# Spilled tiles fetched by ScalarE into eight buffers of their own, gate products held two tiles back, early row gathers dropped

## The chip, the core and the metric

The kernel runs on one core of a Trainium2 chip. The metric is device time in microseconds (us) of one execution. The profile of an execution gives a span (first to last instruction) and, for each engine, what it did and what it waited for. Engines are named as the profile names them: PE (TensorE), ACT (ScalarE), DVE (VectorE), POOL (GpSimd) and SP (SyncE, which only issues transfers here).

## What is computed

Two transformer layers on 256 tokens of width 1024, in float32. Each layer has a mixing part (convolution, windowed attention, grouped attention; not touched here) and a feed-forward part that looks up experts:

```python
def peer_ffn(h, w_q, sub_keys, u, v):
    ...
        idx = jnp.take_along_axis(cand_i.reshape(PEER_CHUNK, PEER_HEADS, n_cand), best_pos, axis=-1)
        g = jax.nn.softmax(best_s, axis=-1).astype(xc.dtype)
        act = jax.nn.gelu(jnp.einsum('cd,chkd->chk', xc, jnp.take(u, idx, axis=0)))
        return jnp.einsum('chk,chkd->cd', g * act, jnp.take(v, idx, axis=0))
```

Each token uses 8 x 16 = 128 of 16384 experts; `u` and `v` are 16384 x 1024. Layer 0 has 512 tokens in this part (256 of x and 256 of the context), layer 1 has 256.

## The kernel before

**Dense and gathered tokens.** Tokens are handled in tiles of 128. In layer 0 three of the four token tiles are dense: for them all 16384 experts are computed, with a gate that is zero for an expert that was not chosen. The fourth tile gathers its experts' rows instead. In layer 1 both tiles are dense and nothing is gathered.

**Expert tiles.** The 16384 experts are 128 expert tiles, numbered e. For each there is an up gemm (`act`: a 128x1024 piece `u` times the tokens, 24 matmuls into a PSUM bank `psu`, then gelu on ACT into a tile `gact`) and a down gemm (`sweep`: activation times gate, then times a piece `v`, into PSUM banks `acc` that stay open over all 128 tiles; 18 matmuls of 512 columns in layer 0, 12 in layer 1). Every operand is split in a high and a low part to keep float32 accuracy: ACT copies the high part (`hi_u`, `hi_v`, `whi`), DVE or POOL subtracts to get the low part (`lo_u`, `lo_v`, `wlo`), and three matmuls replace one.

**Spilling.** While DVE still works out the routing and the gates, PE runs the up gemms of the first tiles. The first 4 (layer 0) or 8 (layer 1) stay in SBUF. The next 42 or 32 are written to DRAM (`spilled`), and the sweep reads them back as `gback`. So in layer 0 tiles 4 to 45, and in layer 1 tiles 8 to 39, come back in the sweep and need no up gemm there; from tile 46 (40) on, up and down gemms alternate.

**The gates.** `gd` in DRAM holds the gates; a block `gr` with the gates of 8 tiles is fetched by ACT's queue, two buffers. `gr0_40` is the block for tiles 40 to 47 of layer 0. In layer 0 a block is 1536 KB in pieces of 512 bytes. The product of activation and gate is the DVE operation on line 793 (`wi` in the code).

**The gathered tile.** `gather_steps` makes a list of 259 steps: 128 gathers of rows of `u` by POOL's queue (`gru`) with a dot product each on DVE, then 128 gathers of rows of `v` (`grv`), each of 512 KB. Each gather is held until a given instruction has run.

**Order.** A scheduler orders the instructions of each engine from the program and its own estimates; each engine then runs its list strictly in order. A DMA is issued by the engine whose list it stands in, and that engine waits there until the DMA's buffer is free.

Of the kernel before, what the change touches and what calls it, by code (L numbers as in the profile page):

```python
# [11 lines left out]
F32 = mybir.dt.float32  # L12
# [5 lines left out]
AF = mybir.ActivationFunctionType  # L18
ALU = mybir.AluOpType
AX = mybir.AxisListType  # L20

P = 128
# [20 lines left out]
EG = 8  # L43
GA = {0: 4, 1: 8}
SPILL = {0: 42, 1: 32}
GEARLY = 8
GLAG = 3
WOV = {0: (0, 1), 1: (1, 1)}
ZAT = (0, 2, 4, 6, 7, 9)
GE0 = 20  # L50


@with_exitstack
def hymba_kernel(ctx: ExitStack, tc: tile.TileContext, a, out):
    nc = tc.nc
    V, S, G, PE = nc.vector, nc.scalar, nc.gpsimd, nc.tensor
# [137 lines left out]
    def hold(ins, after):  # L194

        if after is not None:
            tc.add_manual_dep(ins.ins, after.ins.name,
                              mybir.DependencyInfo(mybir.DependencyClass.Sync, mybir.DependencyReason.DATA),
                              reason="work that would crowd out more urgent work")
# [387 lines left out]
    def peer(l):  # L587
        first = l == 0
        tiles = [0, 1, 2, 3] if first else [0, 1]
        dense = tiles[:3]  # L590
        gath = tiles[3:]
        nt = len(tiles) * P
        nd = len(dense) * P
        nb = nd // TB
        gapool = ctx_peer.enter_context(tc.tile_pool(name=f"ga{l}", bufs=1))

        near = gapool.tile([P, nb, NEAR[l], TB], F32, name=f"near{l}") if NEAR[l] else None
        gd = near, dram.tile([P, nb, NE, TB], F32, name=f"gd{l}")
        h2 = mixed[l]
        h2n = [gapool.tile([P, D], F32, tag="h2n", name=f"h2n{l}{t}") for t in gath]  # L600
        eidx = [gapool.tile([P, P], U32, tag="eidx", name=f"eidx{l}{t}") for t in gath]
        gates = [gapool.tile([P, P], F32, tag=f"gts{t}", name=f"gts{l}{t}") for t in tiles]

        def back(c, raw):
            for g in range(len(gath)):
                ps = bank("x1", f"psbk{l}{c}{g}")
                PE.transpose(ps[:, :P], raw[:, P:2 * P], ident)
                S.activation(h2n[g][:, c * P:(c + 1) * P], ps[:, :P], AF.Copy)

        norm2(l, 1 if first else 0, back if first else None)  # L610

        gelu = []

        def act(e, tag="gact", bufs=GA[l]):
            u = piece(a["u"][l, e], TP, "u", f"u{l}_{e}", G if e < GA[l] + SPILL[l] else V)
            ps = bank("mm", f"psu{l}_{e}")
            gemm_t(ps[:, :nd], u, h2, slice(0, nd))
            ga = gapool.tile([P, 384], F32, tag=tag, name=f"gact{l}_{e}", bufs=bufs)
            gelu.append(S.activation(ga[:, :nd], ps[:, :nd], AF.Gelu_apprx_tanh))  # L619
            return ga  # L620

        with ExitStack() as es:
            rt = es.enter_context(tc.tile_pool(name=f"rt{l}", bufs=1))
            rw = es.enter_context(tc.tile_pool(name=f"rw{l}", bufs=2))
            n = len(tiles)
            tix = rt.tile([P, n, 16, 16], U32, name=f"tix{l}")
            best = rt.tile([P, n, 8, 16], F32, name=f"best{l}")
            pos = rt.tile([P, n, 8, 16], U32, name=f"pos{l}")

            def top16(o, i, st, scratch):  # L630
                V.max(out=o[:, 0:8], in_=st)
                V.max_index(out=i[:, 0:8], in_max=o[:, 0:8], in_values=st)
                V.match_replace(out=scratch, in_to_replace=o[:, 0:8], in_values=st, imm_value=NEG)
                V.max(out=o[:, 8:16], in_=scratch)
                V.max_index(out=i[:, 8:16], in_max=o[:, 8:16], in_values=scratch)

            ada = (x for g in range(2) for x in ada_group(1, g, by_ring("v"), "x2", rw, 1)) if first else iter(())
            for h in range(8):
                tsc = rt.tile([P, n, 2, 16], F32, tag="tsc", name=f"tsc{l}{h}", bufs=2)
                for k in range(2):  # L640
                    hp = 2 * h + k
                    w = piece(a["w_q"][l, hp], TP, "u", f"wq{l}{hp}", G)
                    if first:
                        next(ada, None)
                    key = rw.tile([P, P], F32, tag="key", name=f"key{l}{hp}", bufs=2)
                    nc.scalar.dma_start(key, a["keys"][l, hp])
                    ps = bank("mm", f"psq{l}{hp}")
                    for o in range(0, nt, T):
                        gemm_t(ps[:, o:o + T], w, h2, slice(o, o + T))
                    q = rw.tile([P, 512], F32, tag="qs", name=f"q{l}{hp}", bufs=3)  # L650
                    S.activation(q[:, :nt], ps[:, :nt], AF.Copy)
                    ps2 = bank("x0", f"pssc{l}{hp}")
                    for t in tiles:
                        ts = slice(t * P, (t + 1) * P)
                        PE.matmul(ps2[:, ts], lhsT=q[:, ts], rhs=key, start=True, stop=True)
                    s = rw.tile([P, 512], F32, tag="qs", name=f"s{l}{hp}", bufs=3)
                    S.activation(s[:, :nt], ps2[:, :nt], AF.Copy)
                    for t in tiles:
                        s2 = rw.tile([P, P], F32, tag="s2", name=f"s2{l}{hp}{t}")
                        top16(tsc[:, t, k, :], tix[:, t, hp, :], s[:, t * P:(t + 1) * P], s2)  # L660
                cand = rw.tile([P, n, 112], F32, tag="cand", name=f"cand{l}{h}")
                V.tensor_tensor(cand[:, :, 0:64].rearrange("p t (i j) -> p t i j", j=16),
                                tsc[:, :, 0, 0:4, None].to_broadcast([P, n, 4, 16]),
                                tsc[:, :, 1, None, :].to_broadcast([P, n, 4, 16]), ALU.add)
                V.tensor_tensor(cand[:, :, 64:112].rearrange("p t (i j) -> p t i j", j=4),
                                tsc[:, :, 0, 4:16, None].to_broadcast([P, n, 12, 4]),
                                tsc[:, :, 1, None, 0:4].to_broadcast([P, n, 12, 4]), ALU.add)
                for t in tiles:
                    top16(best[:, t, h, :], pos[:, t, h, :], cand[:, t], cand[:, t])

            for _ in ada:
                pass
            for t in gath + dense:
                route(l, t, rt, rw, best[:, t], pos[:, t], tix, gates[t], gd if t in dense else None,
                      eidx[gath.index(t)] if t in gath else None)


            early = [act(e) for e in range(GA[l])]
            ns = SPILL[l]
            spilled = dram.tile([P, ns, nd], F32, name=f"spilled{l}")  # L680
            steps = gather_steps(l, gath, h2n, eidx, gates, gapool)
            n_steps = len(steps)
            for e in range(ns):
                nc.sync.dma_start(spilled[:, e, :], act(GA[l] + e, "gsp", 2)[:, :nd])
                while steps and n_steps - len(steps) < GEARLY * (e + 1 - GE0) // (ns - GE0):
                    steps.pop(0)(gelu[-1])

        def act_of(e):
            if e < GA[l]:
                return early[e]  # L690
            if e >= GA[l] + ns:
                return act(e)
            ga = gapool.tile([P, 384], F32, tag="gact", name=f"gback{l}_{e}", bufs=GA[l])
            nc.sync.dma_start(ga[:, :nd], spilled[:, e - GA[l], :])
            return ga

        sweep(l, dense, gath, act_of, h2n, eidx, gates, gd, nd, nb, steps)
# [81 lines left out]
    def sweep(l, dense, gath, act, h2n, eidx, gates, gd, nd, nb, steps):  # L779
        sw = ctx_peer.enter_context(tc.tile_pool(name=f"sw{l}", bufs=2))  # L780
        acc = [[bank(f"x{j}", f"acc{l}{j}{h}") for h in range(2)] for j in range(len(dense))]
        ng = len(steps)
        ahead = GA[l] + SPILL[l]
        gr = None
        rows = None
        last = []
        for e in range(NE):
            ga = act(e)
            if e % EG == 0 and e >= NEAR[l]:
                gr = sw.tile([P, nb, EG, TB], F32, tag="gr", name=f"gr{l}_{e}")  # L790
                nc.scalar.dma_start(gr, gd[1][:, :, e:e + EG, :])  # L791
# [1 line left out]
            wi = V.tensor_tensor(ga[:, :nd].rearrange("p (b t) -> p b t", t=TB),  # L793
                            ga[:, :nd].rearrange("p (b t) -> p b t", t=TB), g, ALU.mult)
            whi = sw.tile([P, 384], F32R, tag="whi", name=f"whi{l}_{e}")
            wlo = sw.tile([P, 384], F32R, tag="wlo", name=f"wlo{l}_{e}")
            S.activation(whi[:, :nd], ga[:, :nd], AF.Copy)  # L797
            V.tensor_tensor(wlo[:, :nd], ga[:, :nd], whi[:, :nd].bitcast(F32), ALU.subtract)  # L798
            v = piece(a["v"][l, e], [P, D], "v", f"v{l}_{e}")

            def down_proj(j, h, e=e, whi=whi, wlo=wlo, v=v):
# [169 lines left out]
```

## Time and profile before

| | us |
|---|---|
| three runs | 2819.54, 2819.16, 2809.11 (median 2819.16) |
| the profiled execution | 2810.39 |
| its span | 2808.6 |
| PE busy | 2647.3 (94% of the span) |
| DVE busy | 1875.9 (67%) |
| ACT busy | 1204.6 (43%) |
| POOL busy | 1036.4 (37%) |

The profiled execution is one execution; what lies around its span is 1.8 us. Matmuls are pipelined, so a busy PE is not a PE at its peak: its work is better counted by matmuls. In the table by windows, the granted clock of PE is given as a share of full speed, and the DMA column is the mean busy share of the 16 DMA engines. In layer 0 the sweep over spilled tiles lies between about 780 and 1000 us from the span's start, in layer 1 between about 2200 and 2300 us.

### The profile page before, as it was taken

Reading aid. Unit: us, or ns where it says so; the run is one execution under the profiler, and the core shown is the slowest. Engines: PE = TensorE matmul, PEld = TensorE weight load, DVE = VectorE, ACT = ScalarE, POOL = GpSimd, SP = SyncE. Lnnn points to the kernel's source line nnn. Section 1 sums busy time; section 2 is a strip of 40 time slices with the busy share of each in tenths; the row PEclk is TensorE's granted clock in tenths of the full one; section 3 lists DMA queues with packets and bytes.
Section 4 is the critical chain, followed back from the end, with each engine's and each line's share of the span. In section 5 each row is a group of like instructions: output and inputs, shape, how many; then the busy total and the mean of one; then the engine's idle time right before and its main releaser. Section 6 shows DMA issues by size and latency. Waiting matters only on the chain. (4 is left out here: it accounts for less than half of the span.)

```text
span 2808.6 us, 41046 instructions
## 1 busy us (share of the span) xinstructions
PE 2647.3 (94%) x15205; PEld 2269.6 (81%) x15205; DVE 1875.9 (67%) x3375; ACT 1204.6 (43%) x1835; POOL 1036.4 (37%) x999
## 2 busy tenths in 40 slices
PE   7999999899898899999999998899899999999998
PEld 4655788799876689989898897558799778999997
DVE  1934599987355667878887865746977665555555
ACT  3335524367322233333333334344466444444444
POOL 4614334665531235444444515424878200000000
PEclk9999999999999999999999999899999999999999
DMA  7353463466877879999998953333468876767663
GB/s 253 100 180 105 164 231 116 141 225 242 282 266 238 259 264 327 339 317 327 328 343 294 345 202 109 127 116 101 141 216 293 273 240 208 218 200 222 209 218 120
DMA packets 264472, 624.67 MB, mean 222 GB/s; under 512 B 22944, under 2 KB 135120, under 8 KB 261200
## 3 DMA queue, kind: packets, MB, share of 16 engines
q1 hardware_dynamic: 138688, 441.15, 46.9%
q0 software_dynamic: 36864, 134.23, 13.2%
q10 hardware_dynamic: 88720, 46.68, 6.0%
q8 instruction: 119, 1.95, 0.3%
q14 instruction: 81, 0.66, 0.1%
HBM read 566.51 MB, written 54.42 MB: 221 GB/s over the span
## 5 line engine op out<-in xcount | busy, mean ns | idle before, releaser
L111 PE MATMUL psu<-ahi_m,hi_u 128*128 128x384 f32 (+1 forms) x2048 | 640.7, 313 | 22.4 <-ACT gact L619 22.4
L113 PE MATMUL psu<-ahi_m,lo_u 128*128 128x384 f32 (+1 forms) x2048 | 643.3, 315 | 11.1 <-POOL lo_u L96 9.1
L112 PE MATMUL psu<-alo_m,hi_u 128*128 128x384 f32 (+1 forms) x2048 | 639.1, 312 | 0.0
L112 PE MATMUL acc<-lo_v,whi 128*128 128x512 f32 x1280 | 507.3, 399 | 27.3 <-DVE lo_v L91 27.2
L91 DVE TENSOR_TENSOR lo_v<-raw_v,hi_v 128x1024 fp32r<-128x1024 f32 x256 | 314.5, 1228 | 220.3 <-ACT hi_v L89 210.8
L111 PE MATMUL acc<-hi_v,whi 128*128 128x512 f32 x1280 | 443.3, 394 | 6.8 <-ACT whi L797 5.5
L113 PE MATMUL acc<-hi_v,wlo 128*128 128x512 f32 x1280 | 445.3, 397 | 0.0
L96 POOL TENSOR_TENSOR lo_u<-raw_u,hi_u 128x256 fp32r<-128x256 f32 x344 | 368.0, 1102 | 188.5 <-ACT hi_u L89 169.9
L111 PEld LDWEIGHTS psu<-ahi_m,hi_u 128*128 128x128 f32 x2048 | 390.3, 191 | 34.2 <-ACT gact L619 24.1
L113 PEld LDWEIGHTS psu<-ahi_m,lo_u 128*128 128x128 f32 x2048 | 390.7, 191 | 25.4 <-POOL lo_u L96 14.8
L89 ACT ACTIVATE hi_v<-raw_v 128x1024 fp32r<-128x1024 f32 x256 | 270.1, 1055 | 316.8 <-PE acc L113 305.6
L112 PEld LDWEIGHTS psu<-alo_m,hi_u 128*128 128x128 f32 x2048 | 391.3, 191 | 6.5
L89 ACT ACTIVATE hi_u<-raw_u 128x1024 fp32r<-128x1024 f32 x256 | 270.6, 1057 | 242.1 <-PE psu L113 119.7
L112 PEld LDWEIGHTS acc<-lo_v,whi 128*128 128x128 f32 x1280 | 244.6, 191 | 82.2 <-DVE lo_v L91 36.0
L872 POOL DMA_INDIRECT gru<-in_u_rows,eidx x128 | 185.2, 1447 | 309.8 <-DVE gback L793 150.7
L111 PEld LDWEIGHTS acc<-hi_v,whi 128*128 128x128 f32 x1280 | 239.8, 189 | 53.4 <-ACT whi L797 7.4
L113 PEld LDWEIGHTS acc<-hi_v,wlo 128*128 128x128 f32 x1280 | 242.2, 191 | 47.7 <-DVE wlo L798 0.3
L872 POOL DMA_INDIRECT grv<-in_v,eidx x128 | 170.2, 1330 | 198.9 <-DVE gact L793 85.6
L91 DVE TENSOR_TENSOR lo_u<-raw_u,hi_u 128x1024 fp32r<-128x1024 f32 x170 | 208.5, 1226 | 41.9 <-ACT hi_u L89 39.8
L797 ACT ACTIVATE whi<-gact 128x256 fp32r<-128x256 f32 (+1 forms) x182 | 84.6, 466 | 323.3 <-DVE gact L793 284.7
L838 POOL TENSOR_TENSOR y<-res,fg 128x512 f32<-128x512 f32 x2 | 2.5, 1264 | 595.7 <-DVE res L569 594.4
L860 DVE SCALAR_TENSOR_TENSOR gru<-gru,h2n 128x1024 f32<-128x1024 f32 x128 | 155.9, 1234 | 83.0 <-DMA gru<-in_u_rows,eidx 61.5
(258 smaller groups left out, 4427.6 us busy)
## 6 DMA issues: line engine op xcount, KB each, us to landing
raw_u<-in_u SPq DMA_DIRECT2D x256, 512.0 KB, 4.5
raw_v<-in_v SPq DMA_DIRECT2D x256, 512.0 KB, 4.4
ada<-in_ada SPq DMA_DIRECT2D x96, 512.0 KB, 4.6
gd<-stage SPq DMA_DIRECT2D x24, 1024.0 KB, 4.8
gr<-gd ACTq DMA_DIRECT2D x16, 1536.0 KB, 17.8
raw_wq<-in_w_q SPq DMA_DIRECT2D x32, 512.0 KB, 3.9
gd<-stage SPq DMA_DIRECT2D x16, 960.0 KB, 5.3
gr<-gd ACTq DMA_DIRECT2D x15, 1024.0 KB, 9.9
```

The costliest lines, as they stand in the source:

```text
L89: S.activation(hi, raw, AF.Copy)
L91: V.tensor_tensor(lo, raw, hi.bitcast(F32), ALU.subtract)
L96: lo_eng.tensor_tensor(lo[sl], raw[sl], hi[sl].bitcast(F32), ALU.subtract)
L111: return [PE.matmul(o, lhsT=ahi, rhs=bhi, start=first, stop=False), PE.matmul(o, lhsT=ahi, rhs=blo, start=False, stop=False), PE.matmul(o, ...
L112: PE.matmul(o, lhsT=ahi, rhs=blo, start=False, stop=False),
L113: PE.matmul(o, lhsT=alo, rhs=bhi, start=False, stop=last)]
L797: S.activation(whi[:, :nd], ga[:, :nd], AF.Copy)
L838: G.tensor_tensor(y[1], resid[t][:, 512:], fg[:, 512:], ALU.mult)
L860: return V.scalar_tensor_tensor(r, r, 1.0, h2n[g], op0=ALU.mult, op1=ALU.mult, accum_out=dots[:, s:s + 1])
L872: d = G.indirect_dma_start(out=r, out_offset=None, in_=a["v_rows" if k >= P else "u_rows"], in_offset=bass.IndirectOffsetOnAxis(ap=eidx[g] ...
```

## The change

Three parts. The reads of spilled tiles move from SP's queue to ACT's, into eight buffers of a pool of their own (before, they shared the 4 or 8 buffers of `gact` with the up gemms). The gate product of a spilled tile e is held until the low part `wlo` of tile e-2 is done (both on DVE). And the eight gather steps that ran beside the spilling up gemms are no longer issued there: all 259 are left to the sweep, whose formula spreads them over its tiles.

```diff
-GEARLY = 8
 GLAG = 3
+GB = 8
...
-GE0 = 20
...
             for e in range(ns):
                 nc.sync.dma_start(spilled[:, e, :], act(GA[l] + e, "gsp", 2)[:, :nd])
-                while steps and n_steps - len(steps) < GEARLY * (e + 1 - GE0) // (ns - GE0):
-                    steps.pop(0)(gelu[-1])
-
-        def act_of(e):
+
+        def act_of(e, sw):
             if e < GA[l]:
                 return early[e]
             if e >= GA[l] + ns:
                 return act(e)
-            ga = gapool.tile([P, 384], F32, tag="gact", name=f"gback{l}_{e}", bufs=GA[l])
-            nc.sync.dma_start(ga[:, :nd], spilled[:, e - GA[l], :])
+            ga = sw.tile([P, 384], F32, tag="gback", name=f"gback{l}_{e}", bufs=GB)
+            nc.scalar.dma_start(ga[:, :nd], spilled[:, e - GA[l], :])
             return ga
...
-            ga = act(e)
+            ga = act(e, sw)
...
-            V.tensor_tensor(wlo[:, :nd], ga[:, :nd], whi[:, :nd].bitcast(F32), ALU.subtract)
+            los.append(V.tensor_tensor(wlo[:, :nd], ga[:, :nd], whi[:, :nd].bitcast(F32), ALU.subtract))
+            if GA[l] <= e < ahead and e >= 2:
+                hold(wi, los[e - 2])
```

The scheduler makes new lists from this. Three places matter for what follows; names are as in the code with layer and tile number (`gback0_37`: tile 37 of layer 0), a last number that only counts tiles, and lines of the changed kernel are a few lower (its gate product is line 788, its gate block line 786, its fetch of a spilled tile line 688).

ACT in layer 0, around the gate block of tiles 40 to 47. Before, it stands between the work for tiles 28 and 29 and no other DMA is near it:

```order
L797 ACTIVATE whi0_28_8504<-gback0_28_8501 128x384
L89 ACTIVATE hi_v0_28_8510<-raw_v0_28_8508 128x1024
L791 DMA gr0_40_8904<-gd0_2569 128x24x128
L797 ACTIVATE whi0_29_8538<-gback0_29_8535 128x384
L89 ACTIVATE hi_v0_29_8544<-raw_v0_29_8542 128x1024
```

The same place in the changed kernel:

```order
L792 ACTIVATE whi0_29_8517<-gback0_29_8514 128x384
L88 ACTIVATE hi_v0_29_8523<-raw_v0_29_8521 128x1024
L688 DMA gback0_37_8782<-spilled0_5988 128x384
L786 DMA gr0_40_8883<-gd0_2569 128x24x128
L792 ACTIVATE whi0_30_8548<-gback0_30_8545 128x384
L88 ACTIVATE hi_v0_30_8554<-raw_v0_30_8552 128x1024
L688 DMA gback0_38_8816<-spilled0_5988 128x384
```

One fetch of a spilled tile now stands behind the work of each tile, eight tiles ahead of its use, and the gate block has one of them directly before it and the next one tile behind it.

DVE in layer 0, where the changed kernel works on tile 31:

```order
L793 TENSOR_TENSOR wlo0_30_8549<-gback0_30_8545,whi0_30_8548 128x384
L788 TENSOR_TENSOR gback0_32_8613<-gback0_32_8613,gr0_32_8615 128x384
L90 TENSOR_TENSOR lo_v0_30_8555<-raw_v0_30_8552,hi_v0_30_8554 128x1024
L857 SCALAR_TENSOR_TENSOR gru0320_8511,dots03_5989<-gru0320_8511,h2n03_2570 128x1024
L788 TENSOR_TENSOR gact0_46_9115<-gact0_46_9115,gr0_40_8883 128x384
L788 TENSOR_TENSOR gact0_47_9177<-gact0_47_9177,gr0_40_8883 128x384
L793 TENSOR_TENSOR wlo0_31_8583<-gback0_31_8579,whi0_31_8582 128x384
L788 TENSOR_TENSOR gback0_33_8649<-gback0_33_8649,gr0_32_8615 128x384
L90 TENSOR_TENSOR lo_v0_31_8589<-raw_v0_31_8586,hi_v0_31_8588 128x1024
```

The products of tiles 46 and 47 stand here, ahead of the low parts of tile 31, and they read the gate block `gr0_40` of the rows above. Before, they stand behind the low parts of tiles 42 and 43. The products of tiles 48 and 49 stand in the same way ahead of the low parts of tile 39, with `gr0_48`, which ACT issues behind its work for tile 37. In layer 1 the eight products of tiles 40 to 47 stand together ahead of the low parts of tile 31.

ACT in layer 1, around the two gate blocks of tiles 40 to 55 in the changed kernel:

```order
L792 ACTIVATE whi1_29_20842<-gback1_29_20839 128x256
L88 ACTIVATE hi_v1_29_20848<-raw_v1_29_20846 128x1024
L688 DMA gback1_37_21041<-spilled1_18930 128x256
L786 DMA gr1_40_21149<-gd1_16682 128x16x128
...
L88 ACTIVATE hi_u1_51_21738<-raw_u1_51_21736 128x1024
L786 DMA gr1_48_21599<-gd1_16682 128x16x128
L688 DMA gback1_39_21091<-spilled1_18930 128x256
L792 ACTIVATE whi1_32_20919<-gback1_32_20914 128x256
```

Before, `gr1_48` stands between the work for tiles 32 and 33 with no DMA behind it; now a fetch and the whole work of tile 32 stand directly behind it.

On PE the count of matmuls is the same. Before, only the up gemms of tiles 46 and 47 stand between the down gemms of spilled tiles in layer 0, up to tile 14; now those of tiles 46 to 51 do, five or six matmuls beside each of tiles 5 to 34, and none beside tiles 35 to 45. In layer 1 the up gemms of tiles 40 to 49 stand beside tiles 7 to 29, and none beside tiles 30 to 39.

## Rows read from the trace of the kernel before

**Rows 1.** Busy time by windows: engines' busy us (instructions), granted clock, DMA share, GB/s.

```profile
780.00:1000.00 220.00, 193.03 (x796) 155.79 (x797) 131.74 (x191) 65.06 (x88) 55.91 (x39) 0.94 0.77 252
1100.00:1200.00 100.00, 100.00 (x506) 90.64 (x505) 80.23 (x118) 35.20 (x48) 50.84 (x36) 1.00 0.95 339
...
2200.00:2300.00 100.00, 97.51 (x475) 79.94 (x474) 64.06 (x94) 47.55 (x70) 3.85 (x4) 1.00 0.82 264
```

**Rows 2.** The same windows, down gemms (`acc`) alone: PE, PEld, DVE.

```profile
780.00:1000.00 220.00, 180.87 (x718) 142.18 (x719) 0.00 (x0) 0.94 0.77 252
...
1100.00:1200.00 100.00, 52.94 (x217) 40.08 (x216) 0.00 (x0) 1.00 0.95 339
```

**Rows 3.** The same windows, up gemms (`psu`) alone: PE, PEld, ACT.

```profile
780.00:1000.00 220.00, 16.38 (x78) 13.77 (x78) 1.92 (x4) 0.94 0.77 252
...
1100.00:1200.00 100.00, 53.88 (x289) 50.82 (x289) 5.64 (x12) 1.00 0.95 339
```

**Rows 4.** PE's instructions in order: start us, us.

```profile
905.61 1.52 PE L111 MATMUL acc<-hi_v,whi 128*128 128x512 f32 x6
906.97 0.39 PE L112 MATMUL acc<-lo_v,whi 128*128 128x512 f32 x1
```

**Rows 5.** Waits from 780 to 1000 us: total us, times, longest.

```profile
ACT whi L797 <- PE acc L112: 123.8, 35, 8.7
DVE gback L793 <- DMA gback<-spilled: 69.5, 32, 7.6
...
PE acc L112 <- DVE lo_v L91: 25.0, 11, 4.5
```

**Rows 6.** Waits of SP's queue from 780 to 1000 us.

```profile
SPq L694 <- DVE wlo L798: 113.1, 35, 8.6
```

**Rows 7.** Transfers issued from 780 to 1000 us: count, KB, median us to landing.

```profile
raw_v<-in_v SPq DMA_DIRECT2D x39, 512.0 KB, 4.9
gback<-spilled SPq DMA_DIRECT2D x38, 192.0 KB, 4.7
gr<-gd ACTq DMA_DIRECT2D x4, 1536.0 KB, 15.2
...
gru<-in_u_rows,eidx POOLq DMA_INDIRECT x35, 5.9
```

**Rows 8.** Gate blocks (`gr`) issued from 780 to 1000 us.

```profile
DMA to landing us min/median/max: 11.5/15.2/17.4
```

**Rows 9.** Transfers issued from 2200 to 2300 us.

```profile
gr<-gd ACTq DMA_DIRECT2D x4, 1024.0 KB, 6.5
```

**Rows 10.** Groups by form: busy us, mean ns of one, then idle time before them.

```profile
L91 DVE TENSOR_TENSOR lo_v<-raw_v,hi_v 128x1024 fp32r<-128x1024 f32 x256 | 314.5, 1228 | 220.3 <-ACT hi_v L89 210.8 <-PE psu L113 9.3
...
L89 ACT ACTIVATE hi_v<-raw_v 128x1024 fp32r<-128x1024 f32 x256 | 270.1, 1055 | 316.8 <-PE acc L113 305.6 <-DMA raw_v<-in_v 10.6
...
L793 DVE TENSOR_TENSOR gback<-gback,gr 128x384 f32<-128x384 f32 x42 | 23.8, 570 | 69.6 <-DMA gback<-spilled 69.5
...
L798 DVE TENSOR_TENSOR wlo<-gback,whi 128x384 fp32r<-128x384 f32 x42 | 23.2, 554 | 8.2 <-ACT whi L797 8.2
...
L797 ACT ACTIVATE whi<-gback 128x384 fp32r<-128x384 f32 x42 | 22.0, 525 | 147.9 <-PE acc L112 129.7 <-DMA raw_v<-in_v 9.1 <-DVE gback L793 8.3
...
L793 DVE TENSOR_TENSOR gback<-gback,gr 128x256 f32<-128x256 f32 x32 | 14.6, 455 | 17.2 <-DMA gback<-spilled 17.2
```

**Rows 11.** ACT's instructions in order, start of both sweeps; in brackets its idle time.

```profile
724.81 11.56 ACTq L791 DMA_DIRECT2D gr<-gd  x2
736.49 0.49 ACT L619 ACTIVATE gact<-psu 128x384 f32<-128x384 f32 x1 [10.72 <-issue]
...
2169.87 5.57 ACTq L791 DMA_DIRECT2D gr<-gd  x2
2175.48 4.98 ACTq L824 DMA_DIRECT2D fg<-in_fin_g  x1
2180.58 1.06 ACT L89 ACTIVATE hi_u<-raw_u 128x1024 fp32r<-128x1024 f32 x1 [10.32 <-issue]
```

**Rows 12.** The kernel's DMA issues of the gates, all of the span.

```profile
gr<-gd ACTq DMA_DIRECT2D x16, 1536.0 KB, 17.8
```

**Rows 13.** SP's instructions in order: one fetch of a spilled tile.

```profile
880.85 0.33 SPq L694 DMA_DIRECT2D gback<-spilled  x1
```

More of the change, by code (lines that the diff above doesn't have):

```diff
@@ L610, in peer @@
         norm2(l, 1 if first else 0, back if first else None)
-        gelu = []
         def act(e, tag="gact", bufs=GA[l]):
@@ L618, in act @@
             ga = gapool.tile([P, 384], F32, tag=tag, name=f"gact{l}_{e}", bufs=bufs)
-            gelu.append(S.activation(ga[:, :nd], ps[:, :nd], AF.Gelu_apprx_tanh))
+            S.activation(ga[:, :nd], ps[:, :nd], AF.Gelu_apprx_tanh)
             return ga
@@ L681, in peer @@
             steps = gather_steps(l, gath, h2n, eidx, gates, gapool)
-            n_steps = len(steps)
             for e in range(ns):
                 nc.sync.dma_start(spilled[:, e, :], act(GA[l] + e, "gsp", 2)[:, :nd])
-                while steps and n_steps - len(steps) < GEARLY * (e + 1 - GE0) // (ns - GE0):
-                    steps.pop(0)(gelu[-1])
-        def act_of(e):
+        def act_of(e, sw):
             if e < GA[l]:
@@ L786, in sweep @@
         last = []
+        los = []
         for e in range(NE):
-            ga = act(e)
+            ga = act(e, sw)
             if e % EG == 0 and e >= NEAR[l]:
```

## The prediction

> **What bounds the kernel now.** I read the busy time by windows first. From 1100 to 1200 us, where up and down gemms of layer 0 alternate, PE is busy throughout at full clock; from 780 to 1000 us, where the sweep runs over spilled tiles, it is busy 193.0 of 220 us at a mean granted clock of 0.94, and in layer 1 from 2200 to 2300 us 97.5 of 100 [rows 1]. Busy time flatters PE, so I count matmuls. Six matmuls of a down gemm start in 906.97 - 905.61 = 1.36 us, 0.227 us each [rows 4]. In the full window, 217 of these [rows 2] leave 100 - 49.2 = 50.8 us for 289 matmuls of up gemms [rows 3], 0.176 us each. From 780 to 1000 us the 718 and 78 matmuls [rows 2, 3] are then worth 162.8 + 13.7 = 176.5 us: **43.5 us are lost there**. 27.0 of them are idle time, the rest is lower clock, so a microsecond of PE idle in this stretch costs 43.5 / 27.0 = 1.6 us in all. In layer 1's window 2.5 us are idle; at the same rate 4.0 us are lost.
>
> The waits of the same stretch tell why [rows 5]. PE waited 25.0 us for `lo_v` of DVE, and DVE had waited 69.5 us, 32 times in 42 tiles, for a spilled tile to land before its gate product. SP's queue shows why it lands late: it stood 113.1 us at the fetch of a spilled tile until `wlo` freed one of four buffers [rows 6], and the loads of `v` stand behind it on that queue. From issue to landing a fetch takes 4.7 us at the median [rows 7], and a tile's 18 down matmuls take 18 x 0.227 = 4.1 us, so a fetch issued so late is late at nearly every tile. ACT is not short of time: it waits 123.8 us for PE to give back a `whi` buffer [rows 5], which means that it works one tile ahead of PE.
>
> **What the eight buffers and the hold take away.** The fetch of tile e+8 is issued when `wlo` of e is done and is used by the product two tiles ahead of `wlo`, six tiles later: 6 x 4.1 = 24.6 us against 4.7, or against 17.4 behind a gate block (the longest landing, [rows 8]). The 69.5 us of DVE waits go, SP's 113.1 us go, and `v` is loaded as its own three buffers allow. I count the whole loss as removed, 43.5 + 4.0 = **-47.5 us**. The lower bound is what PE visibly waited for `lo_v`, 25.0 us. The hold itself orders two DVE operations of 0.55 us that lie side by side anyway, and DVE is busy 131.7 of 220 us [rows 1]: nothing.
>
> **What the fetch costs on ACT.** 74 issues at the 0.33 us that one takes on SP [rows 13] stand in ACT's list, one per tile. ACT is busy 65.1 of 220 us [rows 1]; hidden by its wait for PE. Behind each fetch stands the next tile's `whi`; the fetch waits for `wlo` of the tile that ACT has just finished, which DVE does directly after `whi`. Nothing, as long as DVE is not stuck.
>
> **Where DVE gets stuck next.** In the new lists the products of tiles 46 and 47 stand ahead of the low parts of tile 31, and they read gate block `gr0_40`. Take as zero the moment when PE starts tile 28 and ACT may write `whi` 29. ACT needs 0.53 + 1.06 for `whi` and `hi_v` [rows 10] and 0.33 for a fetch, then issues the block at 1.9. It lands 15.2 us later at the median, 11.5 to 17.4 [rows 8]. DVE has then the two products, `wlo` 31, one product and `lo_v` 31 to do: 3 x 0.57 + 0.55 + 1.23 = 3.5 us [rows 10], so `lo_v` 31 is ready at 1.9 + 15.2 + 3.5 = 20.6. PE asks for it after three tiles and six matmuls. With five or six up matmuls beside each tile, a tile is 4.08 + 5.5 x 0.176 = 5.05 us, so that is at 15.2 + 1.4 = 16.5. PE waits 4.1 us (0.4 to 6.3). At tile 39 the same stands with `gr0_48`: no up matmuls there, so PE asks at 12.2 + 1.4 = 13.6, and `lo_v` 39 is ready at 1.9 + 15.2 + 1.14 + 0.55 + 1.23 = 20.0: 6.4 us (2.7 to 8.6). Together 10.5 us idle, with the clock 10.5 x 1.6 = **+16.8 us** (5 to 24).
>
> In layer 1 the block `gr1_40` lands in 6.5 us [rows 9]; narrow DVE products are 0.46 us [rows 10], and I take 0.46 for `whi` and `wlo` too. Issue at 0.46 + 1.06 + 0.33 = 1.85, landed at 8.35, eight products 3.7, `wlo` and `lo_v` 31 1.7: ready at 13.7, asked for after 3 x 2.72 + 0.9 = 9.1. PE waits 4.6 us. Then ACT's list: `gr1_48` needs the buffer that the eighth product frees at 12.0, and the fetch of tile 39 stands directly behind it. What a DMA behind a gate block on ACT's queue costs the trace shows: in layer 1 the second DMA behind two blocks took 4.98 us to issue, and in layer 0 the second of two blocks took some 11 of the 11.56 us that both took, in which ACT did nothing else [rows 11]. So `whi` 32 is done at 12.0 + 0.5 + 5.0 + 0.5 = 18.0, where PE is through with tile 31 at 13.7 + 1.8 = 15.5: 2.5 us more, and 1.4 for `lo_v` 32. Layer 1 in all 8.5 idle, times 1.6 = **+13.6 us** (6 to 20).
>
> The page "DMA: Bandwidth & Descriptors" of the Trainium skill (section "Queues, rings and completion order") says that on each DMA engine the descriptors of one queue are consumed in ring order. By that rule a fetch behind a block starts when the block's descriptors are through; the 4.98 us agree.
>
> **The other blocks.** In layer 0 `gr0_0` has fetches directly behind it; there a block stood before and cost the same hold, so nothing changes (and the wait at the start of layer 1 is split in two, nothing). At `gr0_8` ACT waits for PE in that moment anyway. At `gr0_16`, `gr0_24`, `gr0_32` the next fetch comes a tile later. Bounds: nothing, if the queue is free again after 5 us, as behind layer 1's blocks [rows 11]; 11 us after the issue, less the tile of 5.05 and less about 2 us (my estimate from ACT's 1.9 us of work in a tile of 5.05) that ACT is ahead, so 3.95 x 1.6 = 6.3 us at each of three, 19 us in all. I take +3, nearer to nothing, since the 11 us were seen with two blocks on end.
>
> **The gathers.** Eight gathers leave the time of the spilling gemms, where PE had work, and make the sweep's rate 259/251 of what it was; after tile 46 that is 3.03 instead of 2.94 of them a tile, 0.09 x 512 KB. The DMA engines have a share of 0.95 there with PE full [rows 1]. Below: nothing, since PE stays the bound. Above: all eight at 512 KB and 339 GB/s, 12 us. With the spilled sweep in 197 us instead of 220 (42 x 4.08 + 144 x 0.176), the transfers of 42 tiles (512 + 192 + 192 KB each), 34 gathers and 6 `u` [rows 7], 59 MB, need 300 GB/s, under 339. I take +3 for both.
>
> **Sum.** -47.5 + 16.8 + 13.6 + 3 + 3 = -11.1 us on the profiled execution's 2810.4 us: **2799 us**. That execution lies 9 us under the median of the three runs (2819.2) and on the lowest (2809.1); I forecast against its own time, and 2799 is 0.7% under that median.
>
> **Rivals.** *The blocks land in time* (0.22). If the lists' early products find their block landed, for instance because a calmer SP queue leaves it room, what is given back is 6 us and 2 for the rest: 2810.4 - 47.5 + 8 = 2771. For it speaks 11.5 us among the landings [rows 8], at which tile 31 costs 0.4 us; against it 17.8 us as the median of all sixteen [rows 12].
>
> *The transfers are the bound, and nothing comes of it* (0.20). The bytes are the same and so are the 16 DMA engines; if the stretch is full of transfers, an earlier issue only waits longer. Speaking for it: a block fills the DMA engines, and `v` then lands late. Against it: the share is 0.77 at 252 GB/s where the next stretch has 0.95 at 339 [rows 1]. Then 2810. The same page of the Trainium skill, section "Issuing engines are not separate DMA queues", has the rule behind this: starting transfers on another engine saves only issue time. By it the queue alone would give nothing, and the trace agrees so far that an issue is 0.33 us; but what the rows show late here is the buffer.
>
> *Slower: ACT held at every block* (0.18). Each fetch one tile behind a block waits until the block is through, and ACT's compute waits with it. The old row has 11 us, and transfers are denser (300 against 252 GB/s), so 13.1 us; less 5.05 and 2 that is 6.05 us, times 1.6, at `gr0_8`, `gr0_16`, `gr0_24` and `gr0_32`, 39 us instead of the 3: 2799 + 36 = 2835. It eats up the gain from a hold of about 9 us on. Against it: it needs the long hold of the two blocks on end at every single block.
>
> **How the numbers follow.** The forecast has 0.40, with its own range of 2786 to 2812 from the bounds of its waits. The range of all cases is 2768 to 2828: below it about a tenth (half of the first rival), above it about a tenth (half of the last). A change under 0.5%, 14 us, can't be told from none here. Against the median, faster means under 2805: of the forecast 0.28 and the first rival 0.22, together 0.50. Slower means over 2833: most of the last rival's upper half and what I have not seen, 0.16. The rest, 0.34, is no change.
>
> **What would show it.** Right: DVE's wait for `spilled` is near nothing; SP no longer waits for `wlo`; the stretch over spilled tiles of layer 0 shows more than 200 matmuls in each 50 us, except for two waits of DVE for `gr` of 6 to 10 us each, some 40 us apart, with PE waiting behind them; layer 1 shows one such wait and then an issue on ACT of about 5 us. Wrong: no DVE wait for `gr` (first rival), `raw_v` landing late and ACT or DVE waiting for it all through (second), issues on ACT of 5 us and more at every block (third).

## The result, and the profile after

The changed kernel takes 2776.22 us (median of four runs, 2767.12 to 2782.85) against 2814.39 for the kernel before (four runs, 2809.11 to 2819.54): a ratio of 0.987, 95% interval 0.984 to 0.989. It is faster, by 38 us at the medians. The profiled execution after is the slowest of the four, 2782.85 us with a span of 2781.1; against the profiled one before it gains 27.5 us, where the forecast had 11.1.

Where in the program? The first operation on layer 0's finished sums (`dres` from `acc`, first and last start at the end of the row) is a milestone. After and before:

```profile
L567 DVE TENSOR_TENSOR dres<-acc,grow x10: 682/684/692, 1668.5 to 2770.6; 128x512 f32<-128x512 f32 x10
```

```profile
L568 DVE TENSOR_TENSOR dres<-acc,grow x10: 682/684/692, 1696.5 to 2798.1; 128x512 f32<-128x512 f32 x10
```

Layer 0 ends 28.0 us earlier, the kernel 27.5 us: in sum layer 1 gave nothing and took nothing. For layer 0, the windows of the changed kernel (columns as in [rows 1]), all instructions first, then the down gemms, then the up gemms:

```profile
780.00:1000.00 220.00, 207.50 (x944) 176.59 (x943) 132.94 (x190) 71.12 (x97) 55.69 (x38) 0.97 0.79 260
920.00:940.00 20.00, 14.94 (x69) 12.48 (x68) 8.50 (x14) 5.37 (x7) 2.89 (x2) 0.94 0.65 212
980.00:1000.00 20.00, 14.65 (x55) 11.68 (x56) 13.60 (x21) 4.43 (x6) 4.42 (x3) 0.83 0.49 160
1000.00:1600.00 600.00, 598.74 (x3007) 541.03 (x3008) 497.48 (x606) 214.11 (x291) 294.66 (x217) 1.00 0.96 340
```

```profile
780.00:1000.00 220.00, 174.40 (x704) 134.22 (x704) 0.00 (x0) 0.97 0.79 260
...
1000.00:1600.00 600.00, 327.83 (x1362) 254.00 (x1362) 0.00 (x0) 1.00 0.96 340
```

```profile
440.00:720.00 280.00, 164.28 (x835) 150.32 (x836) 16.29 (x34) 0.96 0.51 176
...
780.00:1000.00 220.00, 51.02 (x240) 42.91 (x239) 4.26 (x9) 0.97 0.79 260
...
1000.00:1600.00 600.00, 301.32 (x1644) 288.13 (x1645) 33.01 (x70) 1.00 0.96 340
```

At the forecast's own prices, 0.227 us for a down and 0.176 for an up matmul, 704 and 240 are 202.0 us of work: 18.0 us are lost in the stretch of the spilled tiles, where it was 43.3 by the counts of [rows 2, 3]. The rest of layer 0's sweep, 1000 to 1600 us, was not in the forecast. There the kernel before has these counts (down, then up gemms):

```profile
1000.00:1600.00 600.00, 320.57 (x1316) 246.22 (x1317) 0.00 (x0) 0.99 0.92 322
```

```profile
440.00:720.00 280.00, 165.29 (x863) 151.14 (x864) 16.78 (x35) 0.98 0.56 191
...
1000.00:1600.00 600.00, 304.36 (x1644) 289.65 (x1642) 32.00 (x68) 0.99 0.92 322
```

1316 and 1644 are 588.1 us of work, 11.9 lost; after, 1.5. In the spilling gemms, 440 to 720 us, the changed kernel did 28 matmuls less, 4.9 us. By stretches, lost time after minus before is +4.9 (440 to 720), +4.3 (720 to 780, the start of the sweep), -25.3 and -10.4: -26.5 of the 28.0.

The waits from 780 to 1000 us (total, times, longest), which answer to [rows 5]:

```profile
ACT whi L792 <- PE acc L111: 99.2, 31, 11.4
...
ACT whi L792 <- issue: 20.8, 5, 6.9
DVE gact L788 <- DMA gr<-gd: 19.8, 2, 10.2
...
PE acc L111 <- DVE lo_v L90: 12.5, 3, 6.6
```

DVE's wait for `spilled`, 69.5 us before, is not among the waits of this stretch. The two waits for a gate block are there. DVE's instructions in order show the first (start us, us; idle time and what ended it in brackets):

```profile
936.40 1.03 DVE L788 TENSOR_TENSOR gact<-gact,gr 128x384 f32<-128x384 f32 x2 [10.23 <-DMA gr<-gd]
937.34 0.55 DVE L793 TENSOR_TENSOR wlo<-gback,whi 128x384 fp32r<-128x384 f32 x1
937.93 0.56 DVE L788 TENSOR_TENSOR gback<-gback,gr 128x384 f32<-128x384 f32 x1
938.41 1.22 DVE L90 TENSOR_TENSOR lo_v<-raw_v,hi_v 128x1024 fp32r<-128x1024 f32 x1
```

That is the forecast's chain in its order: two products of tiles 46 and 47, `wlo`, a product, `lo_v` of tile 31.

### The profile page after: what moved, and what is told of

It is laid out like the page before. It is cut to its first block, busy times and chain, and to the rows that moved or that the text cites. A ratio compares the mean times of both kernels' runs of the same rounds, so it can differ in the third digit from the quotient of the medians.

```text
span 2781.1 us, 40976 instructions
## 1 busy us (share of the span) xinstructions
PE 2636.9 (95%) x15205; PEld 2269.0 (82%) x15205; DVE 1864.7 (67%) x3375; ACT 1205.5 (43%) x1835; POOL 1024.5 (37%) x999
## 5 line engine op out<-in xcount | busy, mean ns | idle before, releaser
L112 PE MATMUL psu<-ahi_m,lo_u 128*128 128x384 f32 (+1 forms) x2048 | 642.4, 314 | 17.4 <-POOL lo_u L95 17.4
L111 PE MATMUL acc<-lo_v,whi 128*128 128x512 f32 x1280 | 504.4, 394 | 15.5 <-DVE lo_v L90 15.4
L112 PE MATMUL acc<-hi_v,wlo 128*128 128x512 f32 x1280 | 454.7, 393 | 0.0
L110 PE MATMUL acc<-hi_v,whi 128*128 128x512 f32 x1280 | 430.5, 394 | 4.4 <-ACT whi L792 3.0
L95 POOL TENSOR_TENSOR lo_u<-raw_u,hi_u 128x256 fp32r<-128x256 f32 x344 | 356.7, 1071 | 205.2 <-ACT hi_u L88 174.2
```

What stands on the lines that cost most here:

```text
L95: lo_eng.tensor_tensor(lo[sl], raw[sl], hi[sl].bitcast(F32), ALU.subtract)
L110: return [PE.matmul(o, lhsT=ahi, rhs=bhi, start=first, stop=False), PE.matmul(o, lhsT=ahi, rhs=blo, start=False, stop=False), PE.matmul(o, ...
L111: PE.matmul(o, lhsT=ahi, rhs=blo, start=False, stop=False),
L112: PE.matmul(o, lhsT=alo, rhs=bhi, start=False, stop=last)]
```

## The experiments

Twelve runs were made, each compared with the kernel before on the same chip (its medians there: 2813 to 2816 us). "Lost" is the length of a stretch of layer 0 minus its matmuls at the two prices above, in the profiled execution. "Rows" is what DVE waited for gathered rows (`gru`, `grv`) from 1000 to 1600 us. "Places" is counted in DVE's list: how many instructions a row's use stands behind the gate product that releases its gather, mean over the gathers of tiles 47 to 125. Each "lost", "rows" and "places" is one profile or one list, not a mean of runs.

| kernel | median us | ratio to before (95%) | lost 440-720 | 720-780 | 780-1000 | 1000-1600 | rows us | places |
|---|---|---|---|---|---|---|---|---|
| before (profiled 2810.4) | | | 128.1 | 11.1 | 43.3 | 11.9 | 92.7 | 10.6 |
| after | 2776.2 | 0.984-0.989 | 133.0 | 15.4 | 18.0 | 1.5 | 51.9 | 16.4 |
| after_again | 2771.9 | 0.982-0.989 | 132.9 | 8.7 | 14.6 | 0.8 | 52.5 | 16.4 |
| early_gathers_back | 2794.1 | 0.990-0.996 | 132.9 | 21.8 | 13.3 | 12.0 | 90.2 | 12.9 |
| before_no_early_gathers | 2800.8 | 0.994-0.999 | 128.8 | 6.0 | 43.6 | 3.6 | 73.9 | 12.2 |
| eight_in_spilled | 2787.7 | 0.987-0.993 | 132.9 | 12.1 | 16.0 | 12.8 | 87.9 | 13.3 |
| before_fetch_on_act | 2825.2 | 1.002-1.006 | 132.9 | 12.2 | 50.4 | 5.2 | 81.7 | 10.6 |
| fetch_on_sp | 2779.7 | 0.987-0.990 | 127.2 | 9.5 | 19.6 | 1.6 | 53.2 | 16.4 |
| no_hold | 2829.4 | 1.004-1.007 | 132.9 | 11.8 | 39.5 | 17.3 | 84.4 | 13.0 |
| four_buffers | 2785.7 | 0.987-0.992 | 132.9 | 10.0 | 17.4 | 9.0 | 65.6 | 15.0 |
| hold_layer0 | 2764.6 | 0.979-0.986 | 128.3 | 8.5 | 1.2 | 6.5 | 44.4 | 16.0 |
| hold_longer | 2760.3 | 0.980-0.983 | 135.0 | 10.8 | 0.6 | 5.7 | 46.7 | 16.0 |
| hold_longer_lag4 | 2752.0 | 0.976-0.980 | 132.9 | 12.8 | 0.8 | 2.6 | 15.0 | 16.2 |
| hold_layer0_lag2 | 2822.4 | 1.001-1.004 | 132.9 | 14.2 | 0.6 | 61.8 | 130.9 | 16.2 |

**Which part of the change.** After the result my theory was: the buffers and the hold carry the gain, and the later sweep's 10 us are chance. The rival: the gathers.

> The changed kernel once more, for a comparison on one chip with the three below and for the spread from run to run. Theory: its profiled execution (2783 us) holds one mishap that is chance, a single low part of POOL of 9.7 us beside DVE's 16-bit operations near 553 us, which sends the routing some 8 us behind. If chance, the new profile shows no such low part over 3 us in nearly every case, the sweep's first gate block is issued near 725 us instead of 734, and the median is about 2773. Rival: it belongs to the changed order; then it stands in the new profile at the same place and the median is 2776 to 2783.

> The changed kernel with the eight early gather steps put back (parts one and two of the change alone). Theory: eight buffers with the hold carry the gain, the gathers nothing: 2770 to 2780, within 0.3% of the changed kernel. Rival: the 12.9 us that the sweep behind tile 46 gained come from the gathers' new spacing; then this kernel gives them back and is at about 2788.

```diff
+GEARLY = 8
+GE0 = 20
...
                 nc.sync.dma_start(spilled[:, e, :], act(GA[l] + e, "gsp", 2)[:, :nd])
+                while steps and n_steps - len(steps) < GEARLY * (e + 1 - GE0) // (ns - GE0):
+                    steps.pop(0)(gelu[-1])
```

> The kernel before with only the eight early gather steps left to the sweep (part three of the change alone). Theory: no difference, 2809 to 2820. Rival that the gathers carry part of the gain: about 2801, with no DVE wait of more than 3 us for a gathered row between 1200 and 1660 us.

```diff
                 nc.sync.dma_start(spilled[:, e, :], act(GA[l] + e, "gsp", 2)[:, :nd])
-                while steps and n_steps - len(steps) < GEARLY * (e + 1 - GE0) // (ns - GE0):
-                    steps.pop(0)(gelu[-1])
```

My theory fell in part: the first two parts alone give a ratio of 0.993, and leaving the gathers out carries the rest. With the eight gathers back the kernel takes 22 us longer than without (2794.1 against 2771.9 on one chip) and loses 12.0 us in the later sweep again, and 21.8 instead of 8.7 at the start of the sweep; without them, the kernel before gains 0.1 to 0.6% and loses 3.6 there instead of 11.9 (waits over 3 us remain, the longest of 5.2). The low part of POOL of 9.7 us came again (8.9 us); it is taken up at the end.

**Why eight gathers cost so much.** Either they hold DVE where they run, or their absence moves something later. The table says both: from after_again to early_gathers_back, 13.1 us more are lost from 720 to 780 us and 11.2 more behind 1000. The first loss is at the start of the sweep. There PE waits longer for gelus of ACT (the first of these lines, from 720 to 780 us; ACT had stood 10.4 and 7.6 us at issues) and 3.4 us for a `wlo` that took 6.4; and DVE stands at the dot product of an early row, ahead of the gate products of the first four tiles, which start 11.9 us later. Gathers back, then after_again:

```profile
PE psu L112 <- ACT gact L620: 10.3, 2, 7.5
...
753.39 1.48 DVE L864 SCALAR_TENSOR_TENSOR gru<-gru,h2n 128x1024 f32<-128x1024 f32 x1 [23.83 <-ACT gact L620]
...
754.80 3.57 DVE L795 TENSOR_TENSOR gact<-gact,gr 128x384 f32<-128x384 f32 x4
```

```profile
PE psu L110 <- ACT gact L616: 4.8, 1, 4.8
...
742.91 1.96 DVE L788 TENSOR_TENSOR gact<-gact,gr 128x384 f32<-128x384 f32 x4 [17.89 <-DMA gback<-spilled]
```

Which of these waits the gathers cause, and how, no run parts. Without the other two parts the same eight cost less: 5.1 us at the start of the sweep (11.1 against 6.0), 8.3 behind 1000 us, and 12.5 at the medians. For the later sweep, the next run leaves the early gathers out and moves only the later ones.

> The changed kernel, in which the sweep issues eight more of its gather steps over the spilled tiles and 2.94 instead of 3.03 a tile behind them; no gather in the spilling gemms. Theory (place in DVE's list): behind tile 46 a row's use stands on average 13.3 places behind the gate product that releases its gather, 12.9 with the early gathers back and 16.4 in the changed kernel; so DVE's waits for rows from 1000 to 1660 us are some 90 us (94 with the early gathers, 53 in the changed kernel), PE loses about 10 us there, and the time is about 2781. Rival (what costs is that the eight run among the routing and hold DVE at the start of the sweep): within 4 us of 2772.

```diff
-ng - len(steps) < ng * (4 * e - 3 * min(e, ahead)) // (480 - 3 * ahead)
+ng - len(steps) < 8 * min(e, ahead) // ahead + (ng - 8) * (4 * e - 3 * min(e, ahead)) // (480 - 3 * ahead)
```

2787.7 us, with 12.8 lost in the later sweep and 87.9 us of waits for rows, though no gather ran early, and 12.1 at the start of the sweep instead of 21.8. So the later loss goes with where the rows stand in the list, not with early running. DVE's list shows the difference best in gate products between release and use, on average 1.1 before and 2.0 after. In the kernel before, a row released by the product of tile 78 (`grv034`) is used directly behind the next product; in the changed one a row released by that of tile 79 (`grv033`) is used two products later (counted in instructions these two stand 12 and 11 places behind their release, so they are no example of the mean):

```
L793 TENSOR_TENSOR gact0_79_11474<-gact0_79_11474,gr0_72_10978 128x384
L867 SCALAR_TENSOR_TENSOR h2n03_2570<-grv034_11434,dots03_5989,h2n03_2570 128x1024
```

```
L788 TENSOR_TENSOR gact0_79_11460<-gact0_79_11460,gr0_72_10963 128x384
...
L788 TENSOR_TENSOR gact0_80_11533<-gact0_80_11533,gr0_80_11535 128x384
...
L788 TENSOR_TENSOR gact0_81_11606<-gact0_81_11606,gr0_80_11535 128x384
L864 SCALAR_TENSOR_TENSOR h2n03_2570<-grv033_11491,dots03_5989,h2n03_2570 128x1024
```

DVE's waits for rows from 1000 to 1600 us (total, times, longest), before and after:

```profile
DVE h2n L867 <- DMA grv<-in_v,eidx: 54.2, 33, 7.2
DVE gru L860 <- DMA gru<-in_u_rows,eidx: 38.5, 29, 4.4
```

```profile
DVE gru L857 <- DMA gru<-in_u_rows,eidx: 30.4, 31, 2.5
DVE h2n L864 <- DMA grv<-in_v,eidx: 21.5, 21, 3.0
```

How much PE loses by such waits depends on what stands behind them. PE's own waits for the low part of `u` from 1000 to 1600 us are these two lines in early_gathers_back and eight_in_spilled, and none in after_again:

```profile
PE psu L114 <- DVE lo_u L92: 6.1, 2, 3.1
```

```profile
PE psu L112 <- DVE lo_u L90: 9.6, 2, 6.4
```

The places alone don't set the loss: before_fetch_on_act has the 10.6 places of the kernel before and 81.7 us of row waits, and lost 5.2 us there, not 11.9.

Two more runs change how many row buffers there are (four so far), and so when the next gather may start, while the places stay nearly as they were (16.0 to 16.2).

> The hold extended in layer 0, with three row buffers instead of four. Theory: the waits of DVE for gathered rows, not the bytes, cost the kernel before its 12 us behind tile 46; with a buffer less they grow from 45 to over 100 us, and PE loses 10 to 25 us more than with four: 2775 to 2790, though every transfer is the same. Rival (rows wait off the path): within 4 us of 2764.5.

```diff
-GLAG = 3
+GLAG = 2
```

> The same with five row buffers instead of four and each row used four steps behind its gather (the row buffers lie in the sweep's pool to fit). Theory: in the sweep behind tile 46 what PE loses is DVE waiting for gathered rows (45 us of DVE waits in the profile with the extended hold, one of them 2.7 us, behind which PE lost 4.6 us); with a buffer more the waits fall under 20 us and the time by 4 to 6 us, to about 2757. Rival: the DMA engines, at a share of 0.95, deliver rows at the same rate whatever the buffers; then the waits stay at 40 us and the time at that of hold_longer.

```diff
-GLAG = 3
+GLAG = 4
...
-            steps = gather_steps(l, gath, h2n, eidx, gates, gapool)
...
         sw = ctx_peer.enter_context(tc.tile_pool(name=f"sw{l}", bufs=2))
+        steps = gather_steps(l, gath, h2n, eidx, gates, sw)
```

With three row buffers the waits grow to 130.9 us and the kernel is 58 us slower than its twin with four (hold_layer0, below), every transfer being the same; my 10 to 25 us were far too little. With five, the waits fall to 15.0 us (the rows below) and it is 8 us faster than its twin (hold_longer). The row waits cost time, not the bytes.

```profile
DVE gru L857 <- DMA gru<-in_u_rows,eidx: 10.7, 7, 4.8
DVE h2n L864 <- DMA grv<-in_v,eidx: 4.3, 5, 1.8
```

**The two waits for gate blocks.**

> The changed kernel with the hold extended in layer 0 to the eight tiles behind the spilled ones, so that the products of tiles 46 to 49 stand behind the low parts of tiles 44 to 47 and no longer ahead of those of tiles 31 and 39. Theory: the two waits of DVE for a gate block near 935 and 985 us go, and with them the 16.5 us that PE lost there: about 2760, 16 us under the changed kernel. Rival: something else is late next (the block lands in time now but v or the fetch does not), and less than 6 us comes of it: 2770 or more.

```diff
-            if GA[l] <= e < ahead and e >= 2:
+            if GA[l] <= e < ahead + (EG if l == 0 else 0) and e >= 2:
```

> The extended hold in both layers: in layer 1 the eight products of tiles 40 to 47 no longer stand together ahead of the low parts of tile 31. Theory: what PE lost there in the changed kernel, 3.9 us between 2270 and 2290 us, goes: 2761 beside the 2764.5 of the hold in layer 0 alone, and the profile shows no DVE wait for a gate block over 1 us in layer 1. My recorded price for this place was 13.6 us; then 2751. Rival: the gate product of tile 48 now stands ahead of that of tile 43 and waits for its own block, so nothing is gained: 2764 or more.

```diff
-            if GA[l] <= e < ahead and e >= 2:
+            if GA[l] <= e < ahead + EG and e >= 2:
```

Down and up gemms of the second, in the stretch of the spilled tiles:

```profile
780.00:1000.00 220.00, 187.55 (x781) 146.04 (x782) 0.00 (x0) 1.00 0.85 282
```

```profile
780.00:1000.00 220.00, 50.78 (x239) 42.55 (x237) 4.74 (x10) 1.00 0.85 282
```

0.6 us lost at full clock: the two waits cost 17.4 us there in the first profile after and 14.0 in the second. Of these the hold in layer 0 gave only 7 at the median; 5.7 us more are lost behind 1000 us, most of them at one place in the profile of hold_layer0, where a late row (2.71 us of DVE's idle time) stands ahead of `lo_u`. The matmul that waits for that:

```profile
1031.41 0.69 PE L112 MATMUL psu<-ahi_m,lo_u 128*128 128x384 f32 x1 [3.09 <-DVE lo_u L90]
```

Layer 1's wait is worth 4.3 us at the medians (2764.6 to 2760.3), on two chips, less than their intervals can tell; in the profiles PE's one wait of 3.3 us for `lo_v` there is gone.

**Queue, buffers, hold.**

> The kernel before with its fetches on ACT's queue, nothing else changed (four or eight shared buffers, no hold, early gathers). Theory: the queue gives nothing, the issue waits for the low part as on SP, and now ACT's own work stands behind it: 2810 to 2830. Rival that the queue carries the gain because loads of v are no longer behind fetches: 2795 or less.

> The changed kernel with the fetches of spilled tiles back on SP's queue, the eight buffers and the hold kept. Theory: the buffers carry this part of the gain, the queue nothing, and ACT is rid of its 5.7 to 7.2 us at each fetch behind a gate block: 2768 to 2776. Rival that the queue carries it: SP stands at fetches again, loads of v stand behind them, and the stretch from 780 to 1000 us loses some 20 us more: 2790 or more.

```diff
-            nc.scalar.dma_start(ga[:, :nd], spilled[:, e - GA[l], :])
+            nc.sync.dma_start(ga[:, :nd], spilled[:, e - GA[l], :])
```

(The first of the two has the opposite edit on the kernel before.) The queue alone makes the kernel slower by 0.2 to 0.6%; with the fetches back on SP the changed kernel is some 4 to 8 us slower at the median, a little over what was expected, which the intervals don't separate from nothing. The Trainium skill, page "DMA: Bandwidth & Descriptors", section "Issuing engines are not separate DMA queues", says that starting transfers on several engines saves only the time it takes to start them; the 2825.2 us agree in that the queue alone gained nothing.

> The changed kernel without the hold, with its queue and its eight buffers. Theory: the gate product of tile e+8 then stands up to eight tiles ahead of its low part, directly behind the low part of tile e that frees its buffer, so DVE waits for the fetch again at most tiles, as before: 60 us or more of such waits between 780 and 1000 us, 20 us lost there beside the 14 to 18 of the changed kernel, 2795 to 2825. My recorded price for the hold was nothing; by that 2772 to 2780, with eight buffers alone enough.

```diff
-            if GA[l] <= e < ahead and e >= 2:
-                hold(wi, los[e - 2])
```

> The changed kernel with four buffers instead of eight. Theory: the hold sets how far ahead products run, and two tiles (some 9 us) between issue and use are enough for a fetch of 4.7 us except behind gate blocks: 5 to 10 us over the changed kernel, 2777 to 2785. Rival that eight are needed: 2795 or more, with DVE waits for fetches at most tiles.

```diff
-GB = 8
+GB = 4
```

Without the hold, 39.5 us are lost in the stretch and DVE waits for fetches again (first row): the kernel is slower than before, by a little more than expected. Four buffers with the hold lose 17.4 there, like eight (second row), and are some 10 us behind after, most of it from 1000 us on (9.0 lost, places 15.0). No run has the hold with the old shared buffers, so what a pool of their own gives beside the hold is not shown.

```profile
DVE gback L788 <- DMA gback<-spilled: 52.7, 19, 6.8
```

```profile
DVE gback L788 <- DMA gback<-spilled: 9.2, 3, 4.4
```

## Why the prediction was right and wrong

The profiled execution after, 2782.9 us, lies 16.4 below the forecast and under the forecast's own range. Three terms were too high: the gathers by 13.4 us (+3 against a gain of 10.4), layer 1 by about 9 (+9.6 in sum against nothing), the other blocks by 3. Too low were the start, where 9.2 us lost between 440 and 780 us had no term, and the stretch, by 1.4; 1.5 us of the gain lie outside the windows.

**The stretch of the spilled tiles: right in sum.** The forecast took 43.5 us away and gave 16.8 back at two places, 26.7 in all; measured are 25.3. Of the 43.3 us lost, 0.6 remain when the two waits are gone, and the waits cost 17.4 and 14.0 us in two profiles. But the hold, which the forecast priced at nothing, is what makes the buffers work: the product two tiles ahead of `wlo` is the hold's doing, and without it 39.5 us are lost here.

**The other blocks, +3: nothing.** ACT does stand behind the blocks, as the slower rival had it: the next fetch took 5.7 to 7.2 us to issue behind each of `gr0_16`, `gr0_24` and `gr0_32`. Its instructions around the last (6.31 us):

```profile
881.71 0.55 ACTq L786 DMA_DIRECT2D gr<-gd  x1
...
884.06 6.31 ACTq L688 DMA_DIRECT2D gback<-spilled  x1
890.42 0.53 ACT L792 ACTIVATE whi<-gback 128x384 fp32r<-128x384 f32 x1 [6.03 <-issue]
```

But PE is busy throughout from 880 to 900 us, 93 matmuls as in the 20 us before, and so it is from 800 us on: a hold of 6 us a tile behind the block is covered. The rival's place and price on ACT were there; the point from which it decides was not reached.

**Layer 1, +13.6: mis-sized, 3 to 4 us.** One DVE wait came, of 4.1 us, and PE waited 2.9 behind it, at full clock. The block took some 9 us to land instead of 6.5, but the eight products took 2.77 us instead of 3.7; the fetch behind `gr1_48` took 1.69 us to issue, not the 5.0 that I carried over from the second DMA behind two blocks [rows 11]:

```profile
2267.12 0.53 ACTq L786 DMA_DIRECT2D gr<-gd  x1
...
2279.29 0.53 ACTq L786 DMA_DIRECT2D gr<-gd  x1
2279.85 1.69 ACTq L688 DMA_DIRECT2D gback<-spilled  x1
```

```profile
2276.48 2.77 DVE L788 TENSOR_TENSOR gact<-gact,gr 128x256 f32<-128x256 f32 x8 [4.14 <-DMA gr<-gd]
```

The milestones show a sum of about nothing in layer 1, so about as much was taken away there. PE's waits for `lo_v`, 2.3 us in layer 1's sweep before, are part of it; the rest was not followed to a place, so that the forecast's 4.0 is near may be luck.

**The gathers, +3: the step that failed.** It counted 512 KB more here and there against the rate of the DMA engines, and bounded the effect between nothing and a loss. It never asked whether DVE waits for rows in the kernel before (92.7 us from 1000 to 1600), nor where the new list puts a row's use, nor what the early ones cost at the start of the sweep. In the later sweep, where the forecast had a loss, 10.4 us were gained. Leaving the eight out gained 0.1 to 0.6% alone and 22 us beside the other two parts, half of it at the start of the sweep. The parts without it, forecast at -47.5 + 16.8 + 13.6 + 3 = -14.1 us, measured a ratio of 0.993 (0.990 to 0.996), 19 us at the medians.

**The rivals.** The blocks did not land in time, though that rival's 2771 us is near the time: it would have been right by luck. The transfers were not the bound: hold_longer moves 282 GB/s in the stretch, where it was 252, with 0.6 us lost.

## What to carry to other kernels

When a change drops or moves work on an in-order queue, don't price its bytes alone: look at the waits of the stage where it ran, and count how far behind its release each result is now used. Here eight early gathers went with 13 us lost at the start of the next stage, a mean of 10.6 instead of 16.4 places behind transfers of 7.0 to 7.5 us (median from issue to landing, kernel before) with some 10, and one row buffer less with 58. Buffers help only if the consumer's place in the list uses them: the same eight buffers gave nothing without a two-tile hold (2829.4 us). And the waits that a change leaves at the seam of two stages are the next gain: extending the hold over the seam, and one row buffer more, gives 2752.0 us, a ratio of 0.978 (0.976 to 0.980) to the kernel before.

## What was not expected of the hardware

One low part that POOL computes beside the routing took 9.74 us instead of 0.74 in the profile after (POOL's `lo_u` from 540 to 560 us, min/median/max ns), and at most 1.73 in the profile before:

```profile
L95 POOL TENSOR_TENSOR lo_u<-raw_u,hi_u x6: 735/742/9737, 539.0 to 553.1; 128x256 fp32r<-128x256 f32 x6
```

```profile
L96 POOL TENSOR_TENSOR lo_u<-raw_u,hi_u x10: 728/1230/1729, 538.9 to 558.4; 128x256 fp32r<-128x256 f32 x10
```

Meanwhile DVE ran eight 16-bit operations on end. One of them, after and then before:

```profile
554.17 1.25 DVE L754 TENSOR_TENSOR ohA<-sT,iota_t 128x2048 f16<-128x2048 f16 x1
```

```profile
554.43 1.75 DVE L760 TENSOR_TENSOR ohA<-sT,iota_t 128x2048 f16<-128x2048 f16 x1
```

Where DVE's operations take 1.75 us, POOL's go on beside them at 1.23 us each (median); where they take 1.25 us, POOL's operation ends only when they are over. PE waited 6.7 us for it, its granted clock was at 0.63 on the mean from 556 to 566 us, and from 440 to 720 us PE did 28 matmuls less. The Trainium skill, page "SBUF — State Buffer", section "SBUF: two separate sides", says that DVE (with two SBUF inputs, among other cases) and GpSimd share a pair of ports under an exclusive lock, held for a whole instruction, and that the loser fully blocks. The rows fit that only for one instruction at a time: that POOL stayed out over eight on end in one profile, and not in the other, it does not say, and no run took the cause away. The long low part stands in ten of the fourteen profiles, with 132.9 to 135.0 us lost from 440 to 720 us, and is missing in four, with 127.2 to 128.8: before, before_no_early_gathers, hold_layer0 and fetch_on_sp. What decides it stays open. It may be part of what makes runs of one kernel differ, and of the gap between the gain of the profiled executions and that of the medians.
